# A block whose sums stay in PSUM, and VectorE in written order, in the dense expert phase of a hybrid layer

## The chip, the cores and the metric

The kernel runs on one core of a Trainium2 chip. The time is the device time of one execution in microseconds; the number for a kernel is the median of its runs. A profiled execution is a run of its own: it has a time, and a span from its first to its last recorded instruction.

The engines are called as the profile calls them: PE (TensorE; PEld its weight loads), DVE (VectorE), ACT (ScalarE), POOL (GpSimd, which here only gathers rows) and SP (which issues most transfers).

## The reference

A layer works on 1024 frames of 1024 channels: a mixer of two groups (RG-LRU and S5), an output projection, and then a PEER layer with 16,384 experts of one neuron. What concerns the change is the PEER layer:

```python
s1 = jnp.einsum('thd,kd->thk', q[..., :PEER_HALF], k1)
s2 = jnp.einsum('thd,kd->thk', q[..., PEER_HALF:], k2)
v1, i1 = lax.top_k(s1, PEER_TOPK)
v2, i2 = lax.top_k(s2, PEER_TOPK)
cand = (v1[..., :, None] + v2[..., None, :]).reshape(TOK_BLOCK, PEER_HEADS, PEER_TOPK * PEER_TOPK)
sc, cidx = lax.top_k(cand, PEER_TOPK)
...
act = jax.nn.gelu(jnp.einsum('thkd,td->thk', u_sel, xb))
return jnp.einsum('thk,thkd->td', (g * act).astype(xb.dtype), v_sel)
```

Each frame takes 16 experts for each of 8 heads, so 128 of the 16,384. The sum is added to the residual stream, and a last RMS norm follows.

## The kernel before

The frames form eight blocks of 128. Three blocks (5, 6, 7) are **gathered**: for each of a frame's 128 experts POOL fetches a row of U (`row`, 128 x 1024 floats, 512 KB for the whole block), DVE takes its product with the frame (in the profile `CUSTOM_DVE_ANT_0 row<-row,xg`, followed by a read of the sum), and after the gelu a row of V is multiplied and added to the block's stream (`SCALAR_TENSOR_TENSOR hb<-row,act,hb`). That makes 768 rows. Eight buffers hold rows that are on their way.

The other five blocks (0 to 4, 640 frames) are **dense**: all experts are computed, and a matrix G, zero except for the chosen experts, weighs them. The experts are cut into 128 groups of 128. For each group PE computes the activations of all 640 frames (the *first product*, tiles `ap`, 48 matmuls of 320 columns), and then their product with the group's V for each block (the *second product*, tiles `vp`, six matmuls of 512 columns for a block). Every product is made of three matmuls in float32r: each operand is split into a high part (`uh`, `hh`, `vh`: a conversion on ACT) and a low part (`ul`, `hl`, `vl`: the difference on DVE).

Two stages matter here. In the **building stage** G is made from one-hots (`ohA`, `ohB`, `gp`, stored to `G_d`), and the first products of 93 groups are made ahead and stored to `A_d`. In the **dense phase** the 35 other first products and all second products are made. It goes in 32 *chunks* of four groups. In a chunk:

- `products` makes the first products that fall to the next chunk (mostly one, at the end two), out of U groups that `load_split` brings (`ur`, three buffers `raw` shared with V).
- `prepare`, once for each of four groups (a *quarter*), brings the activations back (`hr`, or `ha` if just made), copies the group's weights out of the chunk's part of G (ACT, `gq`), multiplies (DVE, `hr<-hr,gq`), splits the result (ACT `hh`, DVE `hl`) and loads and splits V (`vr`, ACT `vh`, DVE `vl`). Each of `hh`, `hl`, `vh`, `vl` has four buffers, so that of a chunk must be done with before that of the next is written.
- Blocks 0 and 1 are multiplied one after the other, over the four quarters; blocks 2, 3 and 4 go together, quarter by quarter, with the preparation of the next chunk between.
- Behind its last quarter each block's sum (two PSUM banks, three such pairs in turn) is added to the block's stream by DVE (`add`: `TENSOR_TENSOR h<-h,vp`). In the last chunk a `finish` follows: square and square root on ACT, some small steps and the scaling on DVE, and a store.

All of this is written as generators. A merging layer (`Merge`) keeps a clock of its own for each engine and lets that generator go on which is furthest behind; the gathered rows run as one generator, and `step` tells it how many rows may be taken by then, in proportion to the work written. The Tile scheduler then takes what was written and sets each engine's order anew, by its own estimate of when each instruction can run. Neither is bound to the other: rows written in the dense phase may be placed earlier.

Of the kernel before, what the change touches and what calls it, by code (L numbers as in the profile page):

```python
# [7 lines left out]
F32 = mybir.dt.float32  # L8
# [7 lines left out]
PSUM = bass.MemoryType.PSUM  # L16
DRAM = bass.MemoryType.DRAM

P = 128
# [42 lines left out]
class Merge:  # L62
# [30 lines left out]
    def add(self, gens):  # L93

        t0 = min(self.busy[e] for e in ("DVE", "ACT", "PE"))
        self.ths += [dict(g=g, bias=b, t=t0, e=None, w=None) for b, g in gens]
# [739 lines left out]
ND = 5  # L836
# [4 lines left out]
JC = 4  # L841
# [6 lines left out]
def peer(tc, a, cst, pools, h, ss, mg):  # L848
# [3 lines left out]
    V, S, G, PE = mg.V, mg.S, mg.G, mg.PE  # L852
    ident, iota = cst["ident"], cst["iota"]
    acc = h[:ND]
# [10 lines left out]
    pc = pools.open("pc")  # L865
# [4 lines left out]
    ppa = pools.open("ppa", bufs=2, space=PSUM)  # L870
# [96 lines left out]
    rows = pools.open("rows", bufs=ROWS)  # L967
    gp = pools.open("gp", bufs=2)
    pu = pools.open("pu", bufs=2)
# [288 lines left out]
    pools.close("pk2", "pk", "ppt")  # L1258


    ppv = pools.open("ppv", bufs=3, space=PSUM)
    pv = pools.open("pv", "right", bufs=4)
    phh = pools.open("phh", "right", bufs=4)
    pgg = pools.open("pgg", "right", bufs=1)
    nch = P // JC

    def dense():
# [21 lines left out]
        def weights(c):  # L1289
            gts[c] = pgg.tile([P, TD, JC], F32, name="gt", tag="gt")  # L1290
            nc.sync.dma_start(gts[c], G_d[c])
            mg.dma(1280)
# [18 lines left out]
            dst.append((hh, hl, *load_split(pv, a["v"][:, j], [D], "v")))  # L1311
            yield

        def second(p_, b, t, jj):
            hh, hl, vh, vl = t
            bs = slice(b * P, b * P + P)
            for i in range(2):
                ns = slice(512 * i, 512 * i + 512)
                PE.matmul(p_[:, i], hh[:, bs], vl[:, ns], start=(jj == 0), stop=False)
                PE.matmul(p_[:, i], hl[:, bs], vh[:, ns], start=False, stop=False)  # L1320
                PE.matmul(p_[:, i], hh[:, bs], vh[:, ns], start=False, stop=(jj == JC - 1))
            step(5.2 / JC, kb_c / (ND * JC))

        def add(b, p_):
            V.tensor_tensor(acc[b], acc[b], p_.rearrange("p a b -> p (a b)"), ALU.add)
            if c == nch - 1:
                finish(b, acc[b])
# [2 lines left out]
        kb_c = 0.0  # L1330
        yield from products(late[0])
        weights(0)
        nxt = []
        for j in js[0]:
            yield from prepare(j, nxt)
        for c in range(nch):
            now, nxt = nxt, []
            kb_c = JC * 832 + 320 * (JC - len(late[c]))
            if c + 1 < nch:
                weights(c + 1)  # L1340
                yield from products(late[c + 1])

            for b in range(ND - 3):
                p_ = ppv.tile([P, 2, 512], F32, name="vp", tag="vp")
                for jj, t in enumerate(now):
                    second(p_, b, t, jj)
                    yield
                add(b, p_)
                yield
            ps_ = [(b, ppv.tile([P, 2, 512], F32, name="vp", tag="vp")) for b in range(ND - 3, ND)]  # L1350
            for jj, t in enumerate(now):
                for b, p_ in ps_:
                    second(p_, b, t, jj)
                    yield
                    if jj == JC - 1:
                        add(b, p_)
                        yield
                if c + 1 < nch:
                    yield from prepare(js[c + 1][jj], nxt)

# [7 lines left out]
    def step(t, b):  # L1368

        done[0] += t * rate - b  # L1370
        share[:] = [units0 + done[0] / 512]

    step(0.0, 0.0)
    mg.add([(0.0, dense())])
    mg.run([])
    pools.close("pgg", "phh", "pv", "ppv", "ppa", "pu", "gp", "rows", "pc", "acc", "dram")


def body(tc, a):
# [77 lines left out]
```

## Time and profile before

| | before |
|---|---|
| median of 3 runs | 2841.47 us (2841.17 to 2845.11) |
| the profiled execution's own time | 2838.71 us |
| its span | 2836.9 us |
| busy in the span | PE 91%, DVE 85%, ACT 47%, POOL 39% |
| last building step to first second-product matmul | 1590 to 1635 us |
| second products | 1635 to 2825 us |
| rows by DVE | 768, the last near 2690 us |

A line of a timeline has start, duration, engine, source line, operation, what is written and read, and, in brackets, how long the engine was idle before it and what ended the idle time. A line of waits has who waited for whom, the sum in us, how often, and the longest. Nearly all compute has line L146, the helper that records it, so the tiles' names tell the groups apart. A matmul's end is modelled, so PE's rate is taken from starts or from counts.

### The profile page before, as it was taken

What the parts mean: (1) busy time and instruction counts of PE and PEld (TensorE: products, weight loads), DVE (VectorE), ACT (ScalarE), POOL (GpSimd) and SP (SyncE); (2) the same over time, 40 slices, a digit from 0 to 9 for tenths busy, and PEclk for the clock granted to TensorE, in tenths of its full rate; (3) what the DMA queues carried; (4) which work ended last, traced back from release to release, by engine and by line L of the source; (5) the groups of instructions that cost most, each with busy time, mean ns of one, the idle gap of its engine ahead of it and who ended that gap; (6) DMA issues with size and microseconds to landing.
All of it is one profiled execution on the core that took longest, in us unless ns stands there. A gap on an engine that the chain in (4) does not pass through costs nothing.

```text
span 2836.9 us, 40955 instructions
## 1 busy us (share of the span) xinstructions
PE 2578.9 (91%) x14719; PEld 2320.0 (82%) x14719; DVE 2397.7 (85%) x4567; ACT 1324.2 (47%) x2402; POOL 1108.8 (39%) x777
## 2 busy tenths in 40 slices
PE   6888899888899998999989699999999999999998
PEld 5765788788789998999989678888877878788887
DVE  7786535599999998999979699999998999999954
ACT  5355524322286692957839343333433333333442
POOL 0000000033273646647368544454455665444400
PEclk9898899999999999999999899999999999999999
DMA  4110315366699989999899998898899999888842
GB/s 163 25 30 24 127 52 175 128 231 203 232 347 339 336 271 360 372 325 377 269 405 373 384 348 323 327 328 318 326 345 330 344 338 328 319 322 321 318 151 76
DMA packets 301261, 759.88 MB, mean 268 GB/s; under 512 B 28673, under 2 KB 126273, under 8 KB 295937
## 3 DMA queue, kind: packets, MB, share of 16 engines
q0 software_dynamic: 110592, 402.70, 38.5%
q1 hardware_dynamic: 183584, 343.23, 34.9%
q10 hardware_dynamic: 6880, 11.33, 1.1%
q8 instruction: 116, 1.90, 0.3%
q14 instruction: 89, 0.72, 0.1%
HBM read 667.83 MB, written 88.15 MB: 266 GB/s over the span
## 4 chain that ended last, share of the span: by engine, by line
DVE 39%; PE 24%; DMA 13%; issue 13%; ACT 8%; SPq 1%; POOL 1%; DVEq 0%; ACTq 0%; POOLq 0%
DMA ur<-in_uT_dram 8%; DVE hb L146 8%; PE vp L146 7%; DVE row L146 5%; PE ap L146 3%; PE qp L146 3%; DVE vl L146 3%; PE wop L146 3%; DVE ul L146 3%; DMA A_d<-aa 3%; ACT gq L146 3%; DVE ix L146 2%; ACT ohB L146 2%; DVE oh L146 2%; DVE h L146 2%
## 5 line engine op out<-in xcount | busy, mean ns | idle before, releaser
L1126 POOL DMA_INDIRECT row<-in_peer_u_dram,idx x384 | 561.9, 1463 | 1018.0 <-DVE ix L146 564.1
L1126 POOL DMA_INDIRECT row<-in_peer_v_dram,idx x384 | 544.0, 1417 | 520.0 <-DVE hb L146 407.6
L146 PE MATMUL ap<-xDl,uh 128*128 128x320 f32 x2048 | 655.5, 320 | 41.8 <-ACT aa L146 22.9
L146 PE MATMUL ap<-xDh,ul 128*128 128x320 f32 x2048 | 646.8, 316 | 10.1 <-DVE ul L146 8.5
L146 PE MATMUL ap<-xDh,uh 128*128 128x320 f32 x2048 | 644.6, 315 | 0.0
L146 PE MATMUL vp<-vl,hh 128*128 128x512 f32 x1280 | 510.7, 399 | 52.7 <-DVE h L146 47.9
L146 PE MATMUL vp<-vh,hl 128*128 128x512 f32 x1280 | 507.3, 396 | 0.6 <-DVE hl L146 0.6
L146 PE MATMUL vp<-vh,hh 128*128 128x512 f32 x1280 | 506.4, 396 | 0.0
L146 DVE SCALAR_TENSOR_TENSOR hb<-row,act,hb 128x1024 f32<-128x1024 f32 x384 | 492.0, 1281 | 3.5
L146 DVE CUSTOM_DVE_ANT_0 row<-row,xg 128x1024 f32<-128x1024 f32 x384 | 458.6, 1221 | 9.7 <-DMA row<-in_peer_u_dram,idx 6.1
L146 PEld LDWEIGHTS ap<-xDl,uh 128*128 128x128 f32 x2048 | 392.0, 191 | 44.8 <-ACT aa L146 24.5
L146 PEld LDWEIGHTS ap<-xDh,ul 128*128 128x128 f32 x2048 | 391.7, 191 | 14.4 <-DVE ul L146 11.2
L146 PEld LDWEIGHTS ap<-xDh,uh 128*128 128x128 f32 x2048 | 390.9, 191 | 0.0
L146 PEld LDWEIGHTS vp<-vl,hh 128*128 128x128 f32 x1280 | 245.1, 192 | 116.0 <-DVE h L146 62.3
L146 PEld LDWEIGHTS vp<-vh,hh 128*128 128x128 f32 x1280 | 245.5, 192 | 52.5
L146 PEld LDWEIGHTS vp<-vh,hl 128*128 128x128 f32 x1280 | 245.9, 192 | 51.1 <-DVE hl L146 0.9
L146 ACT ACTIVATE gq<-gt 128x640 f32<-128x640 f32 x128 | 175.6, 1372 | 143.8 <-DVE ha L146 71.9
L146 PE MATMUL gp<-ohB,ohA 128*128 128x128 f32 x1280 | 201.2, 282 | 32.3 <-DVE ohB L146 23.2
L146 ACT ACTIVATE uh<-ur 128x1024 fp32r<-128x1024 f32 x128 | 135.2, 1057 | 184.9 <-DMA ur<-in_uT_dram 179.4
L146 PEld LDWEIGHTS gp<-ohB,ohA 128*128 128x128 f32 x1280 | 182.7, 195 | 38.5 <-issue 18.8
L146 DVE TENSOR_TENSOR vl<-vr,vh 128x1024 fp32r<-128x1024 f32 x128 | 156.3, 1221 | 66.4 <-ACT vh L146 64.5
L146 DVE TENSOR_TENSOR h<-h,vp 128x1024 f32<-128x1024 f32 x160 | 189.6, 1214 | 19.1 <-PE vp L146 18.7
(412 smaller groups left out, 4109.0 us busy)
## 6 DMA issues: line engine op xcount, KB each, us to landing
ur<-in_uT_dram SPq DMA_DIRECT2D x128, 512.0 KB
vr<-in_peer_v_dram SPq DMA_DIRECT2D x128, 512.0 KB
G_d<-gs SPq DMA_DIRECT2D x20, 2048.0 KB
gt<-G_d SPq DMA_DIRECT2D x32, 1280.0 KB
A_d<-aa SPq DMA_DIRECT2D x93, 320.0 KB
hr<-A_d SPq DMA_DIRECT2D x93, 320.0 KB
wqr<-in_wq_dram SPq DMA_DIRECT2D x32, 512.0 KB
S_d<-sc SPq DMA_DIRECT2D x64, 128.0 KB
```

Source lines behind the costliest of these rows:

```text
L146: return fn(*args, **kw)
L1126: G.indirect_dma_start(out=r, out_offset=None, in_=a["peer_v" if at >= P else "peer_u"], in_offset=bass.IndirectOffsetOnAxis(ap=idx[n][:, ...
```

## The change

Three things are done in the dense phase.

1. Block 4's sums stay in PSUM: a tile `total` of two banks takes the matmuls of all 32 chunks, and is added once, at the end. The pool of rotating sums has two pairs in place of three.
2. The last part of a chunk takes blocks 2 and 3 together, quarter by quarter, then the quarter of block 4. An add is written later than the product that it belongs to: it is kept in `due` and written after one or two more second products.
3. The whole phase runs under a manual schedule for DVE: its instructions keep the order in which they were written. The other engines are still ordered by the scheduler.

```diff
-    ppv = pools.open("ppv", bufs=3, space=PSUM)
+    ppr = pools.open("ppr", bufs=1, space=PSUM)
+    total = ppr.tile([P, 2, 512], F32, name="total")
+    ppv = pools.open("ppv", bufs=2, space=PSUM)
...
-        def second(p_, b, t, jj):
+        def second(p_, b, t, first, last):
...
             for b in range(ND - 3):
                 p_ = ppv.tile([P, 2, 512], F32, name="vp", tag="vp")
                 for jj, t in enumerate(now):
-                    second(p_, b, t, jj)
+                    second(p_, b, t, jj == 0, jj == JC - 1)
                     yield
-                add(b, p_)
+                    if due and jj == 1:
+                        add(*due.pop())
+                        yield
+                due.append((b, p_, c))
+
+            ps_ = []
+            for jj, t in enumerate(now):
+                for n in range(2):
+                    if not jj:
+                        ps_.append((ND - 3 + n, ppv.tile([P, 2, 512], F32, name="vp", tag="vp")))
+                    second(ps_[n][1], ps_[n][0], t, jj == 0, jj == JC - 1)
+                    yield
+                    if due:
+                        add(*due.pop())
+                        yield
+                end = c == nch - 1 and jj == JC - 1
+                if jj == JC - 1:
+                    add(*ps_[0], c)
+                second(total, ND - 1, t, c + jj == 0, end)
                 yield
-            ps_ = [(b, ppv.tile([P, 2, 512], F32, name="vp", tag="vp")) for b in range(ND - 3, ND)]
-            for jj, t in enumerate(now):
-                for b, p_ in ps_:
-                    second(p_, b, t, jj)
-                    yield
-                    if jj == JC - 1:
-                        add(b, p_)
-                        yield
+                if jj == JC - 1:
+                    due.append((*ps_[1], c))
+                if end:
+                    add(*due.pop())
+                    add(ND - 1, total, c)
                 if c + 1 < nch:
                     yield from prepare(js[c + 1][jj], nxt)
...
-    mg.run([])
-    pools.close("pgg", "phh", "pv", "ppv", "ppa", "pu", "gp", "rows", "pc", "acc", "dram")
+    with tc.manual_schedule(engines={mybir.EngineType.DVE}):
+        mg.run([])
+    pools.close("pgg", "phh", "pv", "ppv", "ppr", "ppa", "pu", "gp", "rows", "pc", "acc", "dram")
```

How it moves DVE's instructions shows at three places. The first is the end of the building stage (`ISA row,act<-row,xg` is the product with a gathered row, `ISA act` the read of its sum, `ohA` and `ohB` are one-hots, `ul` the low part of U). Before:

```order
L146 TENSOR_TENSOR ohA<-iota,kt 128x512
L146 TENSOR_SCALAR ohB<-iota,kt 128x128
L146 ISA row,act<-row,xg 128x1024
L146 ISA act 128x1
L146 ISA row,act<-row,xg 128x1024
L146 ISA act 128x1
L146 TENSOR_TENSOR ul<-ur,uh 128x1024
L146 TENSOR_TENSOR ohA<-iota,kt 128x512
```

and with the change:

```order
L146 TENSOR_TENSOR ohA<-iota,kt 128x512
L146 TENSOR_SCALAR ohB<-iota,kt 128x128
L146 TENSOR_TENSOR ohA<-iota,kt 128x512
L146 TENSOR_SCALAR ohB<-iota,kt 128x128
L146 TENSOR_TENSOR ul<-ur,uh 128x1024
L146 TENSOR_TENSOR ohA<-iota,kt 128x512
```

The rows between the last one-hots belong to the dense phase as written; they stand there now, two or one at a time, up to the last chunk but one.

The second place is the middle of the dense phase (`h_2375`, `h_2376`, `h_2377` are the streams of blocks 2, 3 and 4, `hb<-row,act,hb` is a V row). Before, from one chunk's last quarters into the next:

```order
L146 TENSOR_TENSOR hl<-hr,hh 128x640
L146 TENSOR_TENSOR vl<-vr,vh 128x1024
L146 TENSOR_TENSOR h_2375<-h_2375,vp 128x1024
L146 TENSOR_TENSOR h_2376<-h_2376,vp 128x1024
L146 TENSOR_TENSOR h_2377<-h_2377,vp 128x1024
L146 TENSOR_TENSOR hr<-hr,gq 128x640
L146 TENSOR_TENSOR vl<-vr,vh 128x1024
L146 TENSOR_TENSOR hl<-hr,hh 128x640
L146 TENSOR_TENSOR ul<-ur,uh 128x1024
```

and with the change:

```order
L146 TENSOR_TENSOR vl<-vr,vh 128x1024
L146 TENSOR_TENSOR h_2375<-h_2375,vp 128x1024
L146 SCALAR_TENSOR_TENSOR hb<-row,act,hb 128x1024
L146 TENSOR_TENSOR hr<-hr,gq 128x640
L146 TENSOR_TENSOR hl<-hr,hh 128x640
L146 TENSOR_TENSOR vl<-vr,vh 128x1024
L146 TENSOR_TENSOR ul<-ur,uh 128x1024
L146 SCALAR_TENSOR_TENSOR hb<-row,act,hb 128x1024 x2
L146 TENSOR_TENSOR h_2376<-h_2376,vp 128x1024
```

The adds of blocks 2 and 3 stand apart with other work between, block 4's is gone, and each `hl` stands right behind the `hr` that it needs by way of ACT.

The third is the end, from the add of block 2 in the last chunk. Before:

```order
L146 TENSOR_TENSOR h_2375<-h_2375,vp 128x1024
L146 TENSOR_TENSOR h_2376<-h_2376,vp 128x1024
L146 TENSOR_SCALAR st<-st 128x1
L146 TENSOR_TENSOR h_2377<-h_2377,vp 128x1024
L146 RECIPROCAL st<-st 128x1
L146 TENSOR_SCALAR st<-st 128x1
```

and with the change:

```order
L146 SCALAR_TENSOR_TENSOR h_2375<-h_2375,st,nf 128x1024
L146 TENSOR_TENSOR h_2376<-h_2376,vp 128x1024
L146 TENSOR_SCALAR st<-st 128x1
L146 RECIPROCAL st<-st 128x1
L146 TENSOR_TENSOR st<-st 128x1 x2
L146 TENSOR_SCALAR st<-st 128x1
L146 TENSOR_TENSOR st<-st 128x1
L146 SCALAR_TENSOR_TENSOR h_2376<-h_2376,st,nf 128x1024
L146 TENSOR_TENSOR h_2377<-h_2377,total 128x1024
```

The three finishes interleaved before; now each is whole before the next add.

More of the change, by code (lines that the diff above doesn't have):

```diff
@@ L1318, in second, with add @@
                 ns = slice(512 * i, 512 * i + 512)
-                PE.matmul(p_[:, i], hh[:, bs], vl[:, ns], start=(jj == 0), stop=False)
+                PE.matmul(p_[:, i], hh[:, bs], vl[:, ns], start=first, stop=False)
                 PE.matmul(p_[:, i], hl[:, bs], vh[:, ns], start=False, stop=False)
-                PE.matmul(p_[:, i], hh[:, bs], vh[:, ns], start=False, stop=(jj == JC - 1))
+                PE.matmul(p_[:, i], hh[:, bs], vh[:, ns], start=False, stop=last)
             step(5.2 / JC, kb_c / (ND * JC))
-        def add(b, p_):
+        def add(b, p_, c):
             V.tensor_tensor(acc[b], acc[b], p_.rearrange("p a b -> p (a b)"), ALU.add)
@@ L1332, in dense @@
         weights(0)
-        nxt = []
+        nxt, due = [], []
         for j in js[0]:
```

## The prediction

> **What bounds the kernel now.** I read the page first, then the busy time by stretch, the waits inside the dense phase, and the order of time at its two ends.
>
> ```profile
> span 2836.9 us, 40955 instructions
> PE 2578.9 (91%) x14719; PEld 2320.0 (82%) x14719; DVE 2397.7 (85%) x4567; ACT 1324.2 (47%) x2402; POOL 1108.8 (39%) x777
> ```
>
> ```profile
> 1500.00:1635.00 135.00, 109.76 (x768) 108.88 (x767) 106.80 (x183) 86.89 (x212) 90.32 (x61) 0.90 1.02 387
> 1675.00:2643.00 968.00, 919.49 (x4371) 780.85 (x4370) 893.48 (x964) 362.52 (x397) 501.66 (x360) 0.98 0.91 330
> 2690.00:2770.00 80.00, 80.00 (x420) 70.81 (x419) 45.04 (x49) 34.29 (x39) 0.00 (x0) 1.00 0.42 143
> 2771.00:2826.00 55.00, 54.72 (x242) 44.92 (x241) 25.73 (x36) 15.33 (x21) 0.00 (x0) 1.00 0.21 68
> ```
>
> Columns of the second fence: stretch, length, busy us (and instructions) of PE, PEld, DVE, ACT, POOL, then granted clock, DMA share, GB/s. Four stretches, four limits. The end of the building stage (1500 to 1635) runs with the DMA full while PE idles 25 us. The 26 full chunks (1675 to 2643, 37.2 us each) have PE at 95% and DVE at 92%, neither alone the limit. From 2690 on POOL gathers nothing and PE alone is the limit.
>
> PE's own floor follows from the last two rows. From 2771 on PE runs second products only: 55 us / 242 = 0.227 us each. The row above it is the mix of a chunk with two first products (96 of 320 columns to 120 of 512), 0.190 us on the mean, so a 320-column matmul takes (216 x 0.190 - 120 x 0.227) / 96 = 0.145 us. A normal chunk of 120 and 48 needs 34.2 us, one with 96 needs 41.1. The 37.2 us thus hold 3 us of waiting, which is all that relief of DVE can win in a chunk.
>
> ```profile
> PE vp L146 <- DVE h L146: 46.0, 26, 4.1
> DVE vl L146 <- ACT vh L146: 45.0, 26, 3.7
> DVE hr L146 <- ACT gq L146: 13.8, 52, 0.3
> DVE hl L146 <- ACT hh L146: 11.0, 14, 1.3
> ```
>
> In those 968 us PE waits once a chunk for an add (46.0 us), and DVE waits mostly for a converted V group (45.0).
>
> **The change, part by part. Front.** Counted in DVE's order, 380 of the 768 rows stood ahead of the first add, and now 330. The 50 rows between (512 KB each, 26 MB) leave the fullest stretch of the DMA.
>
> ```profile
> 985.00:1010.00 25.00, 25.00 (x187) 25.00 (x186) 25.00 (x123) 23.54 (x63) 0.00 (x0) 1.00 0.75 250
> 988.87 5.08 SPq L1219 DMA_DIRECT2D A_d<-aa  x1
> 1590.00:1615.00 25.00, 17.78 (x122) 17.51 (x120) 16.04 (x26) 3.82 (x7) 17.30 (x14) 0.90 1.04 411
> 1590.84 0.37 SPq L1087 DMA_DIRECT2D G_d<-gs  x1
> 1594.20 24.86 SPq L1219 DMA_DIRECT2D A_d<-aa  x1
> 1625.16 1.06 ACT L146 ACTIVATE vh<-vr 128x1024 fp32r<-128x1024 f32 x1 [23.00 <-DMA A_d<-aa]
> ```
>
> Behind a store of G_d, SP's next issue is held 5.08 us where POOL issued no row, and 24.86 us where it issued 14. At the end of building that hold keeps the last A_d store, with it the first V conversion (23.00 us of ACT's waiting), and with that the whole dense start. Without the rows I take a hold of 6 us, near the first row: 18 us off. PE's other idle time from 1500 on (25 in all) shrinks a little: 20 us off, bounds 0 (PE or ACT sets the end anyway) and 25 (all of PE's idle time).
>
> **First chunk.** Its preparation now runs in the written order, one quarter after the other.
>
> ```profile
> 1632.09 0.82 DVE L146 TENSOR_TENSOR ha<-ha,gq 128x640 f32<-128x640 f32 x1
> 1632.95 0.74 ACT L146 ACTIVATE hh<-ha 128x640 fp32r<-128x640 f32 x1 [0.44 <-DVE ha L146]
> 1649.29 1.22 DVE L146 TENSOR_TENSOR h<-h,vp 128x1024 f32<-128x1024 f32 x1
> 2006.30 0.82 DVE L146 TENSOR_TENSOR hl<-hr,hh 128x640 fp32r<-128x640 f32 x1
> 2007.03 1.22 DVE L146 TENSOR_TENSOR ul<-ur,uh 128x1024 fp32r<-128x1024 f32 x1
> 2008.17 1.28 DVE L146 SCALAR_TENSOR_TENSOR hb<-row,act,hb 128x1024 f32<-128x1024 f32 x1
> 2009.37 0.82 DVE L146 TENSOR_TENSOR ha<-ha,gq 128x640 f32<-128x640 f32 x1
> 2014.75 1.21 DVE L146 TENSOR_TENSOR h<-h,vp 128x1024 f32<-128x1024 f32 x1
> 2015.88 2.59 DVE L146 SCALAR_TENSOR_TENSOR hb<-row,act,hb 128x1024 f32<-128x1024 f32 x2
> 2018.51 1.23 DVE L146 CUSTOM_DVE_ANT_0 row<-row,xg 128x1024 f32<-128x1024 f32 x1
> 2019.66 0.08 DVE L146 DVE_READ_ACCUMULATOR2_ANT act<- 128x1 f32 x1
> ```
>
> Prices from start to start: hl, ha, hr 0.74; ul, vl 1.14; an add 1.13; a U row 1.15; a V row 1.20, but 1.31 when another V row follows (2.59 - 1.28), since both write hb. One price is new: where hl stands right behind its hr, DVE waits for ACT's hh between them. The first two rows of this fence give it: 0.82 + 0.04 + 0.74 + 0.03 = 1.63 us from hr's start to hl's earliest start, against 0.74: 0.89 us lost. From the first ha to the first add stand now 8 of 0.74, 5 of 1.14, 12 U rows and 3 such waits (the first is covered by a row): 5.9 + 5.7 + 13.8 + 2.7 = 28 us, against 1649.3 - 1632.1 = 17. So 11 us of the front's gain are given back.
>
> **The chunks.** From the first add of chunk 0 to that of chunk 31 it now takes 2804.2 - 1649.3 = 1154.9 us (the last fence below has the later row). In the new order DVE has in this piece 124 adds (155 before: 31 gone, 35 us), 438 rows (388 before: 182 U, 256 V of which 81 are followed by another V), 248 hr or hl, 156 vl or ul: 140 + 209 + 316 + 184 + 178 = 1027 us. All 124 hl now stand right behind their hr: 124 x 0.89 = 110. Queued behind each such hl are a row, its quarter's vl and the next adds, and PE waits for those; nothing may pass. Two finishes of gathered blocks in one piece on DVE (5 each, priced below) and two hand-overs of act through ACT (an estimate of 1.5 each, a little over that of hh), 13 together. Three chunks with two first products are set by PE, 5 more. Sum 1155. PE's two meetings with DVE in a chunk (block 1's add before block 3 can start; hh freed by block 3) come out at 36.5 us a chunk when I lay the prices end to end, the same as DVE's 36.9 with 14 V rows: no slack, so I add 0.2 to 0.3 a chunk, 7. Result 1162, 7 us longer; bounds 1100 (PE at its floor with a microsecond of waiting each) and 1205 (1.7 more a chunk, below).
>
> **The tail.**
>
> ```profile
> 2804.22 1.22 DVE L146 TENSOR_TENSOR h<-h,vp 128x1024 f32<-128x1024 f32 x1 [1.75 <-PE vp L146]
> 2810.35 1.21 DVE L146 TENSOR_TENSOR h<-h,vp 128x1024 f32<-128x1024 f32 x1
> 2812.78 0.15 DVE L146 TENSOR_SCALAR st<-st 128x1 f32<-128x1 f32 x1 [1.22 <-ACT sqf L146]
> 2814.18 1.28 DVE L146 SCALAR_TENSOR_TENSOR h<-h,st,nf 128x1024 f32<-128x1024 f32 x1
> 2832.11 1.28 DVE L146 SCALAR_TENSOR_TENSOR h<-h,st,nf 128x1024 f32<-128x1024 f32 x1
> ```
>
> One finish takes 2810.35 to 2815.46, 5.1 us, nearly half of it waiting for ACT. Now three stand in a row without overlap: from the add of chunk 31 on, 48 matmuls (10.9) less the last 6 (1.4), three finishes (15.3), and the 3.5 us that follow the last multiply today (2833.4 to 2836.9): 28.4 against 32.7. It is 4 us shorter only because PE will be further ahead of DVE when the last chunk begins; the chain itself is longer.
>
> Sum: -20 + 11 + 7 - 4 = -6 us on the span. The profiled run took 2838.71, 1.8 beyond its span, and the median of the runs is 2841.47, so the forecast is 2835 us. The 31 adds are saved, but the 50 rows come to where DVE already sets the pace, and strict order exposes ACT's part of each quarter.
>
> **Rivals.** *DVE keeps its idle share.* The hand-over waits would replace today's waits instead of adding to the work: 893.48 / 968 = 92% busy. Then the piece takes (1027 + 13) / 0.923 = 1127, 28 less than now: -20 + 11 - 28 - 4 = -41, 2800 us. For it: 45.0 us of vl's waiting should vanish, as vl stands late in its quarter. Against it: a wait in strict order can't be filled. The Trainium skill (Perfetto Trace Analysis, Identifying the Most-Contended Engine) takes occupancy as a fair measure for VectorE and would side with this rival; the stretch where both PE and DVE are above 92% is where the rule says least.
>
> *Loads late (slower).* The next U load is issued when the second quarter's vl frees its buffer; ACT converts it ahead of the fourth hh.
>
> ```profile
> 1664.13 8.03 DMA ur<-in_uT_dram
> 1699.91 8.60 DMA ur<-in_uT_dram
> 1739.13 5.93 DMA ur<-in_uT_dram
> ```
>
> My laid-out chunk gives it 7 us from its issue before the fourth hl waits. At 8.6 us the hl comes 1.7 us late in every chunk, and DVE has no work that may pass: 27 x 1.7 = +46, 2881 us. It decides from a landing of 7 us on; today's landings (this chain of waits) lie on both sides, though now they queue behind larger loads.
>
> *Two rotating sums are too few (slower).* With three pairs PE waited 46.0 us for adds; with two, block 3 can't start before block 1 is added. If DVE comes there late by the two rows ahead of that add (2.5 us), PE's floor becomes 34.2 + 2.5 + 1.2 = 37.9, 1 us over my chunk: +30, 2865 us. The Trainium skill (Perfetto Trace Analysis, Optimizing Tensor Performance) wants independent matmul groups to rotate through banks so that evacuation overlaps; here a third of the rotation is pinned. That rule speaks for this rival.
>
> *The front gains nothing* (PE and ACT set its end, the hold on SP was only seen beside it): +14, 2855 us.
>
> **How the numbers follow.** My forecast 0.45, its own range 2815 to 2858; DVE's idle share kept 0.17; loads late 0.20; two sums 0.08; no gain in front 0.10. About 0.2% (6 us) is what a measurement of this kernel can tell from no change. Faster by more: 0.26 of my case and 0.17; within: 0.14 and half of the last rival, 0.19; slower: 0.05 and the rest, 0.38. The range 2800 to 2872 leaves out half of the first rival and most of the second.
>
> **What would show it.** In the new profile: the longest A_d issue on SP after 1590 under 8 us and the first second-product matmul near 1617; "DVE hl <- ACT hh" some 120 times and about 110 us in all; the adds of one chunk 36 to 37.5 us from the next; DVE, not PE, without idle time of any other kind; the last multiply 15 us behind PE's last matmul. A hold that stays above 15 us, an hl wait near 2 us in each chunk, or chunks near 35 us would each make the prediction wrong, in the direction of the rival named.

## The result, and the profile after

The changed kernel takes **2885.5 us** (2877.9 to 2887.7), the kernel before, run beside it, 2843.2: ratio **1.0144** (95% interval 1.0123 to 1.0165). The forecast was 2835, with a range up to 2872. It is slower, and by more than the range allowed.

The page and the stretches of the changed kernel, to be laid beside those shown of before (columns as there: stretch, length, busy us and instructions of PE, PEld, DVE, ACT, POOL, granted clock, DMA share, GB/s):

```profile
span 2883.1 us, 40958 instructions
PE 2599.1 (90%) x14719; PEld 2327.6 (81%) x14719; DVE 2362.9 (82%) x4536; ACT 1325.6 (46%) x2400; POOL 1115.0 (39%) x777
```

```profile
1500.00:1635.00 135.00, 128.57 (x873) 124.23 (x872) 64.14 (x103) 99.04 (x229) 17.47 (x14) 0.99 0.71 229
1637.20:2851.90 1214.70, 1123.06 (x5277) 947.31 (x5276) 1041.66 (x1166) 439.77 (x480) 608.36 (x433) 0.96 0.87 314
1675.00:2643.00 968.00, 900.38 (x4207) 758.76 (x4206) 823.11 (x945) 351.55 (x382) 482.99 (x344) 0.96 0.88 316
```

The end of the building stage is now PE's: up to 1609, where the dense phase begins on DVE, PE is busy all of the last 109 us, and in the whole stretch POOL has 14 instructions in place of 61. In the same 968 us of full chunks both engines are *less* busy than before: PE 900 (919), DVE 823 (893). They wait for each other more.

The marks that the forecast was built on, in order of time. SP's issues around the last G_d store, then the first `ha` and the first add on DVE, the first second product on PE, the first add of the last chunk, the last matmul and the last multiply:

```profile
1585.43 0.37 SPq L1087 DMA_DIRECT2D G_d<-gs  x1
1588.79 2.47 SPq L1219 DMA_DIRECT2D A_d<-aa  x1
...
1609.20 0.83 DVE L146 TENSOR_TENSOR ha<-ha,gq 128x640 f32<-128x640 f32 x1 [8.90 <-ACT gq L146]
...
1613.25 0.47 PE L146 MATMUL vp<-vl,hh 128*128 128x512 f32 x1 [3.84 <-ACT ha L146]
...
1637.20 1.21 DVE L146 TENSOR_TENSOR h<-h,vp 128x1024 f32<-128x1024 f32 x1
...
2851.95 1.21 DVE L146 TENSOR_TENSOR h<-h,vp 128x1024 f32<-128x1024 f32 x1
...
2864.90 0.39 PE L146 MATMUL vp<-vh,hh 128*128 128x512 f32 x1
...
2878.26 1.28 DVE L146 SCALAR_TENSOR_TENSOR h<-h,st,nf 128x1024 f32<-128x1024 f32 x1
```

| part of the span | before | after | difference | forecast |
|---|---|---|---|---|
| to the first `ha` on DVE | 1632.1 | 1609.2 | -22.9 | -20 |
| first `ha` to first add | 17.2 | 28.0 | +10.8 | +11 |
| first add to that of chunk 31 | 1154.9 | 1214.7 | **+59.8** | **+7** |
| from there to the end | 32.7 | 31.2 | -1.5 | -4 |
| span | 2836.9 | 2883.1 | +46.2 | -6 |

Three of the four terms came out near the forecast. The chunks did not. Of their 59.8 us, 44 lie in the first 27 steps from chunk to chunk (38.75 us each, 37.11 before) and 15.5 in the last four (168.6 against 153.1), most of that in the last one (40.2 against 27.2): rows stand there now, where before all rows were done. In the chunks DVE's groups read as follows, before first (line, engine, operation, names, shapes, count, then busy us and mean ns, then idle time in front of them and what ended it):

```profile
L146 DVE TENSOR_TENSOR h<-h,vp 128x1024 f32<-128x1024 f32 x155 | 183.5, 1214 | 9.5 <-PE vp L146 9.4
L146 DVE CUSTOM_DVE_ANT_0 row<-row,xg 128x1024 f32<-128x1024 f32 x132 | 156.4, 1219 | 0.0
L146 DVE TENSOR_TENSOR vl<-vr,vh 128x1024 fp32r<-128x1024 f32 x124 | 151.4, 1221 | 49.3 <-ACT vh L146 47.5
L146 DVE TENSOR_TENSOR hr<-hr,gq 128x640 f32<-128x640 f32 x90 | 76.0, 844 | 21.0 <-ACT gq L146 20.8 <-DMA hr<-A_d 0.3
L146 DVE TENSOR_TENSOR hl<-hr,hh 128x640 fp32r<-128x640 f32 x90 | 73.8, 820 | 12.6 <-ACT hh L146 12.5
L146 DVE TENSOR_TENSOR hl<-ha,hh 128x640 fp32r<-128x640 f32 x34 | 28.0, 823 | 17.1 <-ACT hh L146 17.1
```

and of the changed kernel:

```profile
L146 DVE CUSTOM_DVE_ANT_0 row<-row,xg 128x1024 f32<-128x1024 f32 x183 | 218.7, 1218 | 0.0
L146 DVE TENSOR_TENSOR vl<-vr,vh 128x1024 fp32r<-128x1024 f32 x124 | 151.1, 1218 | 0.0
L146 DVE TENSOR_TENSOR h<-h,vp 128x1024 f32<-128x1024 f32 x124 | 150.6, 1215 | 42.2 <-PE vp L146 39.9 <-issue 2.2
L146 DVE TENSOR_TENSOR hl<-hr,hh 128x640 fp32r<-128x640 f32 x90 | 74.3, 825 | 89.3 <-ACT hh L146 85.5 <-ACT ha L146 2.9 <-issue 0.8
L146 DVE TENSOR_TENSOR hl<-ha,hh 128x640 fp32r<-128x640 f32 x34 | 28.1, 825 | 29.7 <-ACT hh L146 29.7
```

The same piece of before, for the sums:

```profile
1649.30:2804.20 1154.90, 1102.75 (x5290) 940.15 (x5290) 1021.27 (x1095) 439.07 (x482) 530.89 (x382) 0.98 0.85 307
```

The 31 adds are gone (33 us in their group), and some 50 U rows have come (62 us in theirs). The groups add up to more than the engine's busy time, since most instructions start some 0.08 us before the one ahead of them ends (the `hl` at 2049.79 below lasts 0.82 us, and the next starts 0.74 behind it). DVE's busy time in the piece rises from 1021.3 to 1041.7, by 20 us; its idle time from 133.6 to 173.0, by 39. All of `vl`'s waiting has vanished, and `hr`'s. In their place stand `hl`'s, 89.3 + 29.7 = 119.0 us over 124 instructions (12.6 + 17.1 = 29.7 before), and the adds', 42.2 (9.5 before).

PE's side of the same piece also has two parts. It is busy 1123.1 us in place of 1102.8 for the same matmuls, at a granted clock of 0.96 in place of 0.98, and idle for the rest. Among the runs below, the clock in the 968 us goes from 0.92 in the one with the longest chunks (e2) to 0.99 in the one with the shortest (e15). Which of the two follows from the other no run here shows, so the share of these 20 us in the loss stays open.

How one quarter looks now, and what else is late in the same chunk. The first four lines are one `hl` waiting for ACT, the last three the load of U, its conversion and the first products that need it, on SP, ACT and PE:

```profile
2048.16 0.82 DVE L146 TENSOR_TENSOR hr<-hr,gq 128x640 f32<-128x640 f32 x1
2049.01 0.74 ACT L146 ACTIVATE hh<-hr 128x640 fp32r<-128x640 f32 x1 [1.21 <-DVE hr L146]
2049.79 0.82 DVE L146 TENSOR_TENSOR hl<-hr,hh 128x640 fp32r<-128x640 f32 x1 [0.81 <-ACT hh L146]
2050.53 1.28 DVE L146 SCALAR_TENSOR_TENSOR hb<-row,act,hb 128x1024 f32<-128x1024 f32 x1
...
2047.07 0.33 SPq L1181 DMA_DIRECT2D ur<-in_uT_dram  x1
2051.82 1.06 ACT L146 ACTIVATE uh<-ur 128x1024 fp32r<-128x1024 f32 x1 [0.82 <-DMA ur<-in_uT_dram]
2052.93 0.56 PE L146 MATMUL ap<-xDl,uh 128*128 128x320 f32 x2 [2.84 <-ACT uh L146]
```

The row behind `hl` needs neither `hr` nor `hh`, yet it stands behind the wait. On PE two matmuls of the next first product stand ahead of work that is ready, and PE waits for `uh`. In the 968 us that adds up to

```profile
DVE hl L146 <- ACT hh L146: 93.8, 97, 2.9
PE ap L146 <- ACT uh L146: 62.0, 25, 4.5
DVE h L146 <- PE vp L146: 39.2, 19, 4.9
```

where before PE waited 46.0 us for adds and `hl` 11.0 for `hh`.

### The profile page after: what moved, and what is told of

Read it like the earlier page. It is cut to its first block, busy times and chain, and to the rows that moved or that the text cites. A ratio compares the mean times of both kernels' runs of the same rounds, so it can differ in the third digit from the quotient of the medians.

```text
span 2883.1 us, 40958 instructions
## 1 busy us (share of the span) xinstructions
PE 2599.1 (90%) x14719; PEld 2327.6 (81%) x14719; DVE 2362.9 (82%) x4536; ACT 1325.6 (46%) x2400; POOL 1115.0 (39%) x777
## 3 DMA queue, kind: packets, MB, share of 16 engines
q0 software_dynamic: 110592, 402.70, 38.6%
## 4 chain that ended last, share of the span: by engine, by line
DVE 35%; PE 33%; DMA 12%; issue 12%; ACT 7%; POOL 1%; SPq 0%; ACTq 0%; DVEq 0%; POOLq 0%
PE vp L146 11%; DVE hb L146 7%; PE ap L146 7%; DVE row L146 5%; DMA ur<-in_uT_dram 5%; PE wop L146 3%; PE total L146 3%; PE qp L146 3%; DVE ix L146 2%; DVE vl L146 2%; DVE ul L146 2%; ACT ohB L146 2%; DMA A_d<-aa 2%; DVE oh L146 2%; ACT hh L146 2%
## 5 line engine op out<-in xcount | busy, mean ns | idle before, releaser
L1126 POOL DMA_INDIRECT row<-in_peer_v_dram,idx x384 | 560.0, 1458 | 489.4 <-DVE hb L146 388.9
L146 PE MATMUL vp<-vl,hh 128*128 128x512 f32 x1024 | 405.3, 398 | 11.6 <-DVE vl L146 6.1
L146 PE MATMUL vp<-vh,hl 128*128 128x512 f32 x1024 | 405.2, 396 | 0.0
L146 PE MATMUL vp<-vh,hh 128*128 128x512 f32 x1024 | 405.0, 396 | 0.0
L146 PEld LDWEIGHTS ap<-xDh,ul 128*128 128x128 f32 x2048 | 390.8, 191 | 15.6 <-DVE ul L146 10.9
L146 ACT ACTIVATE vh<-vr 128x1024 fp32r<-128x1024 f32 x128 | 135.9, 1062 | 496.4 <-PE vp L146 435.3
L146 PEld LDWEIGHTS vp<-vl,hh 128*128 128x128 f32 x1024 | 197.9, 193 | 60.5 <-issue 11.7
L146 PEld LDWEIGHTS vp<-vh,hh 128*128 128x128 f32 x1024 | 195.9, 191 | 42.2
L146 PEld LDWEIGHTS vp<-vh,hl 128*128 128x128 f32 x1024 | 197.1, 193 | 40.3
L146 ACT ACTIVATE ohB<-ohB,kt 128x128 f32<-128x128 f32 x480 | 203.7, 494 | 0.0
L146 DVE TENSOR_TENSOR ul<-ur,uh 128x1024 fp32r<-128x1024 f32 x128 | 155.6, 1217 | 46.5 <-ACT uh L146 45.2
```

The source lines that it names most:

```text
L146: return fn(*args, **kw)
L1126: G.indirect_dma_start(out=r, out_offset=None, in_=a["peer_v" if at >= P else "peer_u"], in_offset=bass.IndirectOffsetOnAxis(ap=idx[n][:, ...
```

## The experiments

Each run has its median and its ratio to the kernel before on the same chip. In these runs the kernel before lay between 2822 and 2857 us, so the ratios' intervals (0.2 to 0.5% to either side) are what can be told; 0.2%, which the prediction took for that, was too fine for most of them. Against the ranges written ahead of each run, e1, e6, e10, e12, e13, e14 and e17 came out in one of them or within 2 us of it, e4, e5, e7, e15 and e18 between two, e2, e3, e8, e11 and e16 above all, and e9 below.

| run | edit | median us | ratio, interval |
|---|---|---|---|
| after | the change | 2885.5 | 1.0144, 1.0123 to 1.0165 |
| e1 | without the written order | 2900.2 | 1.0217, 1.0171 to 1.0263 |
| e5 | e1, adds at once | 2867.1 | 1.0100, 1.0053 to 1.0148 |
| e2 | written order alone | 2975.8 | 1.0466, 1.0410 to 1.0523 |
| e3 | after, PE in written order too | 2912.4 | 1.0242, 1.0197 to 1.0287 |
| e4 | after, `vl` between `hr` and `hl` | 2816.6 | 0.9913, 0.9877 to 0.9948 |
| e17 | e3 with e4's edit | 2847.3 | 1.0010, 0.9983 to 1.0038 |
| e6 | e2 with e4's edit | 2824.8 | 0.9953, 0.9930 to 0.9975 |
| e7 | e4, adds at once | 2816.6 | 0.9925, 0.9899 to 0.9951 |
| e9 | e3, 50 rows less | 2823.1 | 0.9942, 0.9917 to 0.9968 |
| e13 | e3, 50 rows gathered, not added | 2854.3 | 1.0060, 1.0027 to 1.0093 |
| e14 | e3, 50 rows added, not gathered | 2916.2 | 1.0252, 1.0211 to 1.0292 |
| e10 | after, four raw buffers | 2857.3 | 1.0055, 1.0033 to 1.0077 |
| e16 | before, four raw buffers | 2872.6 | 1.0116, 1.0073 to 1.0158 |
| e8 | e4, rows paced faster | 2867.6 | 1.0088, 1.0059 to 1.0118 |
| e11 | e8, PE in written order too | 2918.4 | 1.0257, 1.0210 to 1.0305 |
| e12 | e4, last chunk in the scheduler's order | 2809.0 | 0.9889, 0.9845 to 0.9933 |
| e15 | e12, four raw buffers | 2802.3 | **0.9852, 0.9803 to 0.9900** |
| e18 | e15 with three rotating pairs | 2818.2 | 0.9918, 0.9892 to 0.9944 |

### Which part of the change costs

**e1**: the resident sum and the later adds alone.

```diff
-    with tc.manual_schedule(engines={mybir.EngineType.DVE}):
-        mg.run([])
+    mg.run([])
```

> The change without the written order on VectorE: the resident sum and the later adds stay. 380 rows stand ahead of the first add again, as before. Theory A (the written order on VectorE, with what it does to the other engines, costs the chunks their 53 us beyond the forecast): front as before (no 23 us gained), 31 adds of 1.13 us less on VectorE in the chunks, so at or below the kernel before: 2805 to 2842 us. Theory B (two rotating pairs beside the resident sum are too few, whatever the order): the adds still come late for TensorE and the loss stays: 2865 us or more. If the front's 23 us and the written order's cost were all there is, after + 23 - 60 = 2848 us at most.

**e5**: the resident sum alone; e1, and the adds written as in the kernel before.

```diff
-                    if due and jj == 1:
-                        add(*due.pop())
-                        yield
-                due.append((b, p_, c))
+                add(b, p_, c)
...
```

> The resident sum alone: no written order on VectorE, and each block's add written right behind its last matmul, as in the kernel before, not a quarter or a block later. The run without the written order (resident sum and later adds) took 2900, with TensorE waiting 87 us in 968 for adds against 46 before. Theory B1 (the resident sum leaves two rotating pairs, and that is too few for this order, whenever the adds are written): again 2880 to 2915 us, with TensorE waiting over 75 us for adds. Theory B2 (the adds come late because they are written later, behind rows that the scheduler put ahead): TensorE waits at most the 46 us of before, 31 adds less: 2805 to 2845 us.

**e2**: the written order alone, in the kernel before.

```diff
-    mg.run([])
+    with tc.manual_schedule(engines={mybir.EngineType.DVE}):
+        mg.run([])
```

> The kernel before (three rotating pairs, five adds a chunk, adds where they were) with VectorE's instructions of the dense phase kept in the written order. 329 rows ahead of the first add, so the front gains its 20 us here too. Theory A (written order): VectorE has 31 adds more than after, 35 us, and the same waits of hl for ACT's hh (0.98 each): 2895 to 2925 us. Theory B (resident sum): with three pairs the chunks go back to 37.3 us and the front's gain shows: 2815 to 2835 us.

Each part by itself loses, and the losses don't add: +1.0% for the resident sum, another 1.2 for the later adds when the scheduler orders them, +4.7% for the written order alone; both together (after) lose 1.4. The first add stands at 1650.2 in e1 and 1649.0 in e5, as before, and at 1629.6 in e2: the front's gain is the written order's. From the first add to that of chunk 31 it takes 1202.5 us in e1, 1183.1 in e5 and 1318.1 in e2, against 1154.9. The waits in the 968 us, of e1, then e5, then e2:

```profile
PE vp L146 <- DVE h L146: 86.7, 39, 3.6
```

```profile
PE vp L146 <- DVE h L146: 71.4, 31, 3.6
```

```profile
ACT hh L146 <- DVE hr L146: 205.1, 68, 5.8
DVE hl L146 <- ACT hh L146: 151.1, 89, 5.1
PE ap L146 <- ACT uh L146: 119.5, 23, 9.8
```

So the prediction's third rival exists: with two rotating pairs and rows that the scheduler is free to put ahead of an add, PE waits 71 to 87 us for adds where it waited 46. That e5's time is near the 2865 us worked out for it is chance: that sum had the front's gain in it, which e5 lacks. The Trainium skill (Perfetto Trace Analysis, Optimizing Tensor Performance) wants groups of matmuls to rotate through banks; e1 and e5 agree with it. But it is not what the changed kernel suffers from: there PE's wait for adds has gone from the list. Theory A was wrong on e1 (it expected at most 2842) and right on e2's direction, though not on its size.

### TensorE's order

**e3**: the first products' early matmuls put back into one piece.

```diff
-    with tc.manual_schedule(engines={mybir.EngineType.DVE}):
+    with tc.manual_schedule(engines={mybir.EngineType.DVE, mybir.EngineType.PE}):
```

> The changed kernel with TensorE's instructions of the dense phase in the written order too: a first product's 48 matmuls stand in one piece behind the resident sum's last quarter, where now two of them stand ahead of that sum's third quarter and wait for uh. VectorE's order is unchanged. Theory A1 (TensorE waits for uh at the misplaced two, 62 us in 968, and VectorE's adds then wait for TensorE, 39 us): both waits go, 1.5 to 2 us a chunk: 2825 to 2850 us. Theory A2 (VectorE's own strict chain sets the pace, hl 0.98 us behind hr four times a chunk, and TensorE's wait only fills slack): 2880 to 2890 us, no change. Theory C (loads late: V and U raw buffers shared, so uh is late wherever its first user stands): TensorE waits for uh or ul elsewhere, 2870 to 2890 us.

Slower still, and theory A1 falls. PE no longer waits for `uh`, but 67.6 us for adds instead, and DVE's adds still wait for PE:

```profile
PE vp L146 <- DVE h L146: 67.6, 31, 3.2
DVE hl L146 <- ACT hh L146: 112.5, 100, 2.7
...
L146 DVE TENSOR_TENSOR h<-h,vp 128x1024 f32<-128x1024 f32 x125 | 151.9, 1215 | 47.0 <-PE vp L146 47.0
L146 DVE TENSOR_TENSOR hl<-hr,hh 128x640 fp32r<-128x640 f32 x90 | 74.3, 825 | 82.1 <-ACT hh L146 82.1
L146 DVE TENSOR_TENSOR hl<-ha,hh 128x640 fp32r<-128x640 f32 x34 | 28.0, 825 | 55.4 <-ACT hh L146 55.4
```

(The waits are of the 968 us, the groups of the whole piece.) PE's wait has only changed its name, which points to DVE's chain behind it; e9, e13 and e14 test that.

### The hand-over from hr to hl

**e4**: V's load and split written ahead of the split of `hr`, so that `vl` stands between `hr` and `hl`.

```diff
+            v_ = load_split(pv, a["v"][:, j], [D], "v")
+            yield
             hh = phh.tile([P, TD], F32R, name="hh", tag="hh")
             hl = phh.tile([P, TD], F32R, name="hl", tag="hl")
             split_to(hh, hl, hr)
+            dst.append((hh, hl, *v_))
             yield
-            dst.append((hh, hl, *load_split(pv, a["v"][:, j], [D], "v")))
-            yield
```

> The changed kernel with the V load and split of a quarter written ahead of the split of hr into hh and hl: on VectorE vl now stands between hr and hl, so ACT's hh (0.74 us) lies under vl (1.14). TensorE's order changes with it: the first products stand in one piece. Theory A1 (uh waits only): as the run with TensorE in the written order, 2825 to 2850 us. Theory A2 (hl's waits set the pace): 97.6 us of waiting in 968 go, chunks fall from 39 to 35 to 36 us: 2770 to 2800 us, unless vl waits for V's load or conversion in their place, then 2840 to 2885 us.

Faster than after by 2.4%, and than before by 0.9%. In this edit PE's order also changes by itself (its first products come in one piece), so two more runs make the comparison cleaner. **e17** holds PE's order in both: e3 and this edit.

> The changed kernel with VectorE and TensorE in the written order and vl between hr and hl; against the run with both in the written order and hl right behind hr (2912). Theory A2 (the hand-over hr to hh to hl on VectorE sets the pace; 137 us of hl's waits in that run's chunks): 60 to 100 us off, 2815 to 2850 us. Theory A4 (the gain of that edit came from TensorE's order): 2895 to 2915 us.

**e6** has the edit on e2, with three pairs and five adds.

> The kernel before with VectorE's written order (three rotating pairs, five adds a chunk), and the split of V written ahead of that of hr, so that vl stands between hr and hl. With hl right behind hr this kernel took 2976. Theory A (hl's wait for ACT is what makes the written order dear): it falls by more than 100 us, below 2870; 31 adds more than the changed kernel with the same edit (2817) would then be 2825 to 2850 us, or less if the third pair is worth more than the adds. Theory D (the first products' two early matmuls, which wait for uh there, 119.5 us in 968, are the cause): TensorE's order is whole here too, so this run does not exclude it alone; but the changed kernel with TensorE in the written order did not gain from it (2912).

All three gain: 69, 65 and 151 us. DVE's groups for `hl` in the piece, of e4 and then e17 (there up to 2820):

```profile
L146 DVE TENSOR_TENSOR hl<-hr,hh 128x640 fp32r<-128x640 f32 x90 | 73.7, 819 | 47.9 <-ACT hh L146 47.9
```

```profile
L146 DVE TENSOR_TENSOR hl<-hr,hh 128x640 fp32r<-128x640 f32 x91 | 74.5, 819 | 55.1 <-ACT hh L146 55.1
```

against 82.1 + 55.4 in e3 and 89.3 + 29.7 in after; `hl<-ha` no longer waits in either. In after the median of the 124 waits is 0.81 us and none is shorter than 0.8; in e4 107 of the 124 do not wait at all. From the first add to that of chunk 31, e4 is 66 us shorter than after, e17 53 than e3 and e6 157 than e2. The edit also has V's load written earlier, but earlier loads are not what e17 won: in e3 DVE waits 0.0 us in front of `vl` and 0.6 in front of `ul` in the whole piece, PE does not wait for `uh`, and ACT's wait for U in the 968 us is 15.8 us in e3 and 79.2 in e17. One exchange of two lines takes the loss away.

**e7**: e4 with the adds at once instead of later, as in e5's diff.

> The changed kernel with vl between hr and hl (2817) and its adds written at once behind each block's last matmul instead of later. If the later adds are worth something in strict order (VectorE reaches an add only when TensorE has finished the block): adds at once make VectorE wait for TensorE, in each chunk up to some 2 us more: 2840 to 2880 us. If they only delay TensorE (two pairs): 2780 to 2810 us.

No difference (2816.6 both), and neither theory is right. When the adds are written matters in the scheduler's order (e1 against e5), not here.

### Does VectorE set the pace?

**e9**: e3 with the last 50 V rows of the third gathered block left out, their gathers and their additions, so that the sum of that block lacks them.

```diff
-        for k in range(P):
+        for k in range(P - (50 if n == NG - 1 else 0)):
             vb = take()
...
-    left = 2 * NG * P - units0
+    left = 2 * NG * P - 50 - units0
```

> The changed kernel with TensorE in the written order (2912), with the last 50 V rows of the third gathered block left out (their gathers and their additions; the output is then not the reference's there). 12 rows a chunk in place of 14; the orders on VectorE and TensorE are otherwise the same. Theory A2 (VectorE's strict chain sets the pace of every chunk): 50 x 1.2 = 60 us off, 2845 to 2865 us. Theory A3 (the pace is set by the ring of hand-overs between VectorE, ACT and TensorE, the rows fill gaps of it): under 30 us off, 2885 to 2912 us.

It gains 89 us, more than their 60 us on DVE. Each row is also 512 KB on a DMA that is 0.88 busy, so two runs take one half of a row away each. **e13** gathers 50 of the V rows and does not add them (the sums of two blocks lack them); **e14** does not gather them and adds the row before twice in their place.

```diff
+            if n and k % 5 == 4:
+                V.tensor_copy(act[:, k:k + 1], vb[:, 0:1])
+            else:
-            V.scalar_tensor_tensor(hb, vb, act[:, k:k + 1], hb, ALU.mult, ALU.add)
+                V.scalar_tensor_tensor(hb, vb, act[:, k:k + 1], hb, ALU.mult, ALU.add)
```

> The changed kernel with TensorE in the written order (2912); of the second and third gathered block's 256 V rows every fifth (50) is gathered as before, but not added: VectorE only copies one column of it. All orders stay. Theory A2 (VectorE's strict chain sets the pace): 50 x 1.1 = 55 us off and some of the waits behind it, as with 50 rows left out altogether (2823): 2820 to 2860 us. Theory F (the row's 512 KB on the DMA make the other loads late): 2890 to 2915 us.

```diff
+        if n and at >= P and at % 5 == (P + 4) % 5:
+            asked.append(asked[-1])
+            return True
         r = rows.tile([P, D], F32, name="row", tag="row")
```

> The same kernel the other way round: the 50 rows are not gathered (26 MB less), and VectorE adds the row before each of them a second time in its place. VectorE's work and all orders stay. Theory A2 (VectorE's strict chain): no change, 2900 to 2915 us. Theory F (the DMA's load): 2825 to 2870 us.

e13 gains 58 us, and DVE's busy time from the first add to that of chunk 31 falls by 60 (1042.1 to 982.3; 50 x 1.1 = 55 was expected), while its waits stay: `hl` 137.5 us in e3 and 138.5 in e13, the adds 47.0 and 42.6. e14 gains nothing for 26 MB. The 968 us of e13 and of e14:

```profile
1675.00:2643.00 968.00, 923.99 (x4424) 779.77 (x4423) 821.00 (x983) 367.67 (x401) 494.79 (x363) 0.99 0.91 332
```

```profile
1675.00:2643.00 968.00, 898.76 (x4176) 753.51 (x4177) 819.87 (x943) 347.69 (x380) 436.06 (x309) 0.96 0.84 296
```

In e14 the DMA's share falls to 0.84 and the time stays. In e13 it rises to 0.91 and the chunks get shorter. So in strict order DVE's work counts one to one although the engine is busy only 85% of the time: its waits are part of the chain. (PE's granted clock is 0.99 in e13 and 0.96 in e14; as above, whether that follows from the shorter chunks or adds to the gain is open.) The Trainium skill (Perfetto Trace Analysis, Identifying the Most-Contended Engine) takes occupancy for a fair measure on this engine; here 15% of its time was idle, and yet all the work that was taken away came off the total.

In e9 the waits shrink as well, the adds' from 47.0 to 24.5 us and `hl`'s from 137.5 to 131.6: 28 of the 31 us that it wins beyond e13. Why they shrink is not settled. e9's rows are left out evenly, and e9 also drops the gathers that e13 keeps, so that the DMA is excluded as a cause only where DVE's work stays.

### Loads

**e10**: a fourth raw buffer, for which the gathered rows give up one of eight.

```diff
-ROWS = 8
+ROWS = 7
...
-        r = pu.tile([P] + shape, F32, tag="raw", name=tag + "r", bufs=3)
+        r = pu.tile([P] + shape, F32, tag="raw", name=tag + "r", bufs=4)
```

> The changed kernel with four buffers instead of three for the raw U and V loads, and seven instead of eight for the gathered rows (the space is not there otherwise); the written order and TensorE's order stay the same. Theory C (loads late: ur's load is issued only when a vl frees its buffer, uh is late, TensorE waits for uh 62 us in 968 and VectorE for TensorE 39): the U load is issued a quarter earlier, both waits shrink: 2835 to 2865 us. Theory A2 or A3 (the hand-overs hr to hh to hl and the strict chain): uh may come earlier, but the chunks stay at 39 us: 2875 to 2895 us.

**e16** makes the same edit in the kernel before.

> The kernel before with four raw buffers and seven for rows. ACT waits 145 us in 968 there for ur's landing. If the shared raw buffers bind the kernel before just as the changed one: 2805 to 2820 us. If its order lets VectorE fill those waits: 2833 to 2850 us.

After gains 28 us by it; before loses 33 against its neighbour of 2839 us, more than either theory had. Why it loses is not settled: ACT's wait for U falls there from 145.3 to 110.3 us in the 968, but PE's wait for adds rises from 46.0 to 62.6, and the rows have one buffer less. In e10's piece, 1187.2 us long, DVE's adds and `hl`, and a new wait of PE in the 968 us:

```profile
L146 DVE TENSOR_TENSOR h<-h,vp 128x1024 f32<-128x1024 f32 x125 | 152.1, 1217 | 8.2 <-PE vp L146 8.2
L146 DVE TENSOR_TENSOR hl<-hr,hh 128x640 fp32r<-128x640 f32 x90 | 74.3, 826 | 97.0 <-ACT hh L146 94.1 <-ACT ha L146 1.5 <-ACT vh L146 1.4
...
PE total L146 <- DVE vl L146: 36.0, 25, 3.5
```

The adds' wait for PE falls from 42.2 to 8.2 us; `hl`'s does not fall. PE's 62.0 us for `uh` are gone from its list, and PE waits 36.0 us for `vl` instead. So the second new wait of the changed kernel comes from U's late load, by way of `uh` and PE. That holds for the order that PE has there: in e3, where PE does not wait for `uh`, the adds wait 47.0 us all the same.

### Rows away from the end, and what beats both

**e8**: e4, with the rows' pace raised by 6%, so that none is left for the last two chunks.

```diff
-        done[0] += t * rate - b
+        done[0] += 1.06 * t * rate - b
```

> The changed kernel with vl between hr and hl (2817), and the rows paced 6 per cent faster, so that they end with chunk 28 instead of the last: 15 rows in a chunk in place of 14, none in the last two. If rows spread to the end cost time there (the last four steps took 174 us against 153 before): 15 to 20 us off, 2795 to 2803 us. If VectorE sets the pace in all chunks alike, the rows only change place: 2812 to 2820 us. If the extra row a chunk (1.2 us) makes VectorE late in the full chunks: 2820 to 2840 us.

**e11**: the same with PE in the written order.

> The changed kernel with vl between hr and hl and rows paced 6 per cent faster (2868), and TensorE in the written order as well. In that run the order on TensorE had changed by itself: the resident sum's quarters b to d had come to stand behind block 0, and TensorE waited there for hh (33.6 us in 968). If that reordering cost the 51 us: with TensorE's order as written the run comes to 2795 to 2820 us. If the extra row a chunk cost them (VectorE late): 2850 to 2875 us.

Both are slower, by 51 us against e4 and 71 against e17. The last chunks did become shorter (the last step 29.8 and 30.1 us against 38.6 and 38.8), but the first 27 steps longer, 39.0 us on the mean in e8 against 36.1 in e4, for one row more. DVE is not busier by it, it waits more: in the 968 us it works 860.2 us in e8 and 837.2 in e11, against 880.1 and 858.5. In e11 these are the longest waits between DVE and PE:

```profile
PE vp L146 <- DVE h L146: 84.0, 40, 7.4
DVE hl L146 <- ACT hh L146: 61.9, 19, 4.4
DVE h L146 <- PE vp L146: 29.8, 20, 2.9
```

Which of the moved rows makes which add late was not traced. That a written order is this sensitive to one row a chunk stays an observation.

**e12**: e4, with the written order ending before the last chunk.

```diff
+            if c == nch - 1:
+                mg.flag("last")
             now, nxt = nxt, []
...
     with tc.manual_schedule(engines={mybir.EngineType.DVE}):
-        mg.run([])
+        mg.run([], until="last")
+    mg.run([])
```

> The changed kernel with vl between hr and hl (2817), VectorE's written order kept up to the last chunk only, whose instructions the scheduler orders. In strict order the finishes of the last blocks stand in a row, each with 2 us of waiting for ACT; from TensorE's last matmul to the end it takes 17.6 us, against 11.2 in the kernel before. If that is strict order's cost: 6 us off, 2807 to 2813 us. If TensorE's end moves later for it (rows or adds in another order): 2815 to 2825 us.

From PE's last matmul to the end it takes 11.2 us again (17.6 in e4), and the median falls by 8 us, of which this explains 6; the intervals overlap.

**e15** adds e10's buffers to e12.

> The changed kernel with vl between hr and hl and the last chunk in the scheduler's order (2809), and with four raw buffers for U and V and seven for rows. There ACT waited 74 us in 968 for ur's landing, and VectorE 39.5 for hh, which stands behind uh on ACT. If the two cures add: 28 us off again, 2780 to 2795 us. If uh was late only because of the strict chain that is now gone: 2805 to 2812 us.

```profile
1675.00:2643.00 968.00, 937.07 (x4512) 793.99 (x4511) 884.48 (x1009) 376.47 (x411) 537.62 (x371) 0.99 0.93 341
```

2802 us, between the two ranges expected, and the lowest median of all: 1.5% below the kernel before and 2.9% below the changed one. Its interval overlaps those of e12 and e4, so the 7 us that the four buffers seem to win here are not shown. PE is at 97% in the full chunks. **e18** is e15 with three pairs and no resident sum.

> The kernel before with VectorE's written order up to the last chunk, vl between hr and hl, four raw buffers and seven for rows: as the run of 2802, but with three rotating pairs and no resident sum, so five adds a chunk. If 31 adds of 1.13 us are VectorE's pace: 2820 to 2840 us. If the third pair gives as much as the adds cost: 2797 to 2810 us.

16 us slower by the medians (the intervals just overlap): once the hand-over is hidden, the resident sum is worth about half of the 35 us of its 31 adds, by the medians (8 us in e4 against e6).

## Why the prediction was wrong

Point by point, by its own steps:

- **Front, -20: right in size and place.** It came to -22.9; the last A_d issue was held 2.47 us, not 24.86, and the first second product stands at 1613 (1617 forecast). The rows go with it: with 380 of them ahead of the first add, the first V conversion stands at 1625 to 1627 us (before, e1, e5), with 329 or 330 at 1594 to 1600 (e2, after). That the hold is the path is less sure. In e1 it is only 15.48 us, and the conversion, at 1626.81, is no earlier. The terms also partly cancel: the hold is 22.4 us shorter (18 forecast), the last G_d store 5.4 earlier, and 5 of that is lost again before the first `ha`.
- **First chunk, +11: right**, 28.0 us with the 12 rows and the three waits that were laid out.
- **DVE's work in the chunks, 1027 us: right.** 1041.7 us are measured as busy; less the two finishes and hand-overs of act (4.6) and the 0.075 us at the end of each of 124 `hr` or `ha` that the next instruction no longer overlaps (9.3, counted in the hand-over), 1027.8.
- **The hand-over, 124 x 0.89 = 110: right in kind and place, 18 us too small.** 119.0 us of waiting and those 9.3 make 128. 103 of the 124 take what was forecast; 21 wait longer, up to 2.9 us, for an `hh` that came later.
- **"No slack, so I add 0.2 to 0.3 a chunk, 7", and 5 for three chunks with two first products: this step failed.** These 12 us stand against 42.2 of adds that wait for PE, 1.4 a chunk. The meetings of PE and DVE were laid end to end at 36.5 and 36.9 us, each with the other on time. With no slack in either, the lateness of a third party is passed on: PE's two early matmuls wait for `uh` (62.0 us in the 968), and the next add waits for PE. e10 takes 34 of the 42.2 us away by an earlier load. It is not the only way to be late, as e3 shows (47.0 us without a wait for `uh`), and PE's lower clock may have a part in it. That 30 and the 18 above, with some 4 of small waits, are the 53 us between 1162 and 1214.7.
- **Tail, -4: near** (-1.5), and most of the 2.8 us beyond it lies ahead of the finishes: PE's last matmul starts 13.0 us behind the add of chunk 31, where the sum has 10.9. The last multiply starts 13.4 us behind that matmul; the sum has 12.6 there (9.5 + 15.3 - 1.3 - 10.9), its list of signs 15.
- **The rivals.** *DVE keeps its idle share* is wrong: the idle time grew. *Loads late* had the right cause and the wrong path. It had U's load delay the fourth `hh` by 1.7 us a chunk; all waits of `hl` over 0.95 us together are 35.7 us, 19 more than the hand-over alone. But the load delays PE's first products and so the adds, and e10 puts its price at 28 us, not 46. *Two rotating sums* is right in kind for the scheduler's order (e1, e5) and does not show in the written one. *No gain in front* is wrong.

What the experiments add is the weight of the terms. The hand-over was priced as 110 us of waiting inside a sum that came out even; that made it look paid for by the adds and by waits that vanish. e4 and e17 show that it is worth 65 to 69 us of the whole time, more than the change loses. The forecast had its main term right; the term for the meetings of PE and DVE was a surcharge with no row of the profile behind it, and it held next to nothing for a load that comes late.

## What to carry to other kernels

An instruction order that is fixed by hand is worth what its worst neighbours are worth: look for each pair in which an instruction needs a round trip through another engine from the one right ahead of it, and put independent work of at least that length between (here `vl`, 1.14 us, over 0.81). In such a chain an engine can be the bound at 85% busy, so test it by taking work away, not by its share. And where two engines' chains come out at the same length, do not forecast the sum of either: give the lateness of every load that one of them waits for a price of its own (here 62.0 us of PE's waiting for `uh`, of which an earlier load won 28).

## What was not expected of the hardware

Taking 26 MB of transfers away moved nothing (e14), although the DMA was 0.88 busy: its share fell to 0.84. Taking one buffer of eight from the gathered rows and giving it to the loads won 28 us in the changed kernel and lost 33 in the kernel before, with the same work on every engine in both.
